# The adaLN pieces' quadrant sums by a two-column product, and three banks for the first mixer's pieces

## The chip, the cores and the metric

One Trainium2 chip; the kernel runs on one core of it. The metric is device time in microseconds of one execution, lower is better. TensorE (PE) does the matmuls and the transposes, VectorE (DVE), ScalarE (ACT) and GpSimd (POOL) the rest; every DMA that matters here is issued from SyncE's queue (SP).

## The reference

Two layers of a hybrid backbone block over 512 tokens (256 context, 256 latent) of width 1024. Layer 0 mixes with gated linear attention (GLA) next to an mLSTM, layer 1 with a Mamba-2 scan, and each is followed by a convolutional SwiGLU network (FFN). Every norm is modulated by adaLN: a conditioning vector (one for the latent, one for the context) goes through SiLU and one large product per layer, and that gives a shift, a scale and a gate for the mixer and the same for the FFN.

```python
def rmsnorm(x, g):
    xf = x.astype(jnp.float32)
    y = xf * lax.rsqrt(jnp.mean(xf * xf, axis=-1, keepdims=True) + EPS)
    return (y * g.astype(jnp.float32)).astype(x.dtype)

def modulate(x, g, shift, scale):
    return rmsnorm(x, g) * (1 + scale) + shift
```

## The kernel before

**Products.** The 1024 features lie in eight blocks of 128. Each large product is done in three passes of fp32r, high·high, low·high and high·low (L180 to L182 where the result has features on partitions, L215 to L217 where it has tokens there). Weights come as raw fp32 in transfers of 1 MB (`Stream`, L140 to L175, DMA at L154): ACT copies the raw half into `wh` (L168), and DVE, or POOL in the FFN, subtracts to get `wl` (L169). Raw tiles live in two slots, so a third transfer is issued when the first tile has been read by its last reader. PSUM is split into three pools: `gps` with 4 banks for the products, `mps` with 3 for the mixers, `vps` with 1.

**adaLN pieces.** The modulation is computed in pieces of 512 columns (`mod_chunk`, L230), 20 of them, and in 8 smaller ones of 256 (`mod_part`, L243, at the start). A piece issues two raw transfers of 1 MB (L236) into the *same* two raw slots as the weights, and does eight fp32 matmuls with the silu vector `spad` as the stationary operand (L239): each writes 32 rows of a bank, so that four quarters of the contraction lie in four quadrants of partitions. Then `mod_out` (L253): ACT copies the bank into `t2` (L256), PE transposes each block of 128 columns against `ident` (L259; 4 for a piece, 2 for a part), DVE adds the four quadrants (L263), adds the bias (L264), and for the scales applies the gain (L267). Both the bank of the products and that of the transposes come from the pool `psa`, by default `vps`, the single bank; L127 (column sums of squares of the norm) and L135 use it too.

**Where the pieces stand.** Six pieces of layer 0 (`fill0`: j = 4, 5, 8, 9, 6, 7) run inside the first mixer: the weight stream calls one when it starts a new raw tile. Two more are in that mixer's gates; the other twelve are for layer 1 and are spread over the rest, nine of them in the first FFN. The mixer itself goes in this order: gate products and the mLSTM's scans (L519 to L530, on 4 partitions, DVE), products of tokens (L215 to L217), then for each pair of GLA heads scores by level (L597, combined on DVE by L603), sums over the state (L672, normalised by L676 to L678), a transposition back (L684), and meanwhile products by features (L180 to L182) whose results DVE puts through a causal convolution (L336, L337, L575). These products wait for `wl`, and so for raw transfers.

**Order.** Nobody writes the order by hand: a scheduler orders each engine's instructions by the dependences and by when slots and banks come free in its own plan. The names in rows and lists are pool and number (`vps_252` is one use of the bank of `vps`; `rawm_253` the raw tile of a piece, `raw_273` one of the weights). On the engine, instructions run strictly in that order.

Of the kernel before, what the change touches and what calls it, by code (L numbers as in the profile page):

```python
# [9 lines left out]
F32 = mybir.dt.float32  # L10
# [3 lines left out]
ALU = mybir.AluOpType  # L14
AX = mybir.AxisListType

P = 128
# [34 lines left out]
def block_kernel(ctx: ExitStack, tc: tile.TileContext, A: dict, out: bass.AP):  # L52
    nc = tc.nc
    PSUM = bass.MemoryType.PSUM
    v, s, g, te = nc.vector, nc.scalar, nc.gpsimd, nc.tensor
# [5 lines left out]
    cp = ctx.enter_context(tc.tile_pool(name="cp", bufs=1))  # L61
# [12 lines left out]
    def nm(b):  # L74
        _u[0] += 1
        return f"{b}_{_u[0]}"

    def t2(shape=(P, T), dt=F32):
        return np_.tile(list(shape), dt, tag="t2", name=nm("t2"), bufs=6)
# [11 lines left out]
    def load(src, shape, dt=F32, eng=None):  # L91
        n = nm("c")
        t = cp.tile(shape, dt, tag=n, name=n)
        (eng or nc.scalar).dma_start(out=t, in_=src)
        return t
# [5 lines left out]
    def pc(name, i=0, n=1):  # L101
        o = _off[name] + i
        return prm[:, o:o + n]
# [121 lines left out]
    v.tensor_scalar(out=cth, in0=cth, scalar1=0.5, scalar2=0.5, op0=ALU.mult, op1=ALU.add)  # L225
    v.tensor_tensor(out=spad[:, :, 0:2], in0=cth.rearrange("p (k c) -> p k c", c=2), in1=cv.rearrange("p (k c) -> p k c", c=2), op=ALU.mult)
    ident = load(A["ident"], [P, P])
    comps = [[cp.tile([P, KD, 2], F32, tag=f"mod{l}_{i}", name=f"mod{l}_{i}") for i in range(6)] for l in range(2)]

    def mod_chunk(l, j, pool=rawp, psa=vps, tag="raw", n=2, bufs=None):  # L230

        ps = psa()
        w = KD // n
        for i in range(n):
            raw = pool.tile([P, w * 512], F32, tag=tag, name=nm("rawm"), bufs=bufs)
            nc.sync.dma_start(out=raw, in_=A["modw"][l, j, :, i * w * 512:(i + 1) * w * 512])  # L236
            for kk in range(w):
                k = i * w + kk
                te.matmul(out=ps[32 * (k % 4):32 * (k % 4) + 32, :], lhsT=spad[:, k, :], rhs=raw[:, kk * 512:(kk + 1) * 512],  # L239
                          start=k < 4, stop=k >= 4)  # L240
        mod_out(l, 4 * j, 4, ps, psa)

    def mod_part(q, pool, psa):  # L243

        ps = psa()[:, :256]
        raw = pool.tile([P, 2048], F32, tag="raw", name=nm("rawm"))
        nc.sync.dma_start(out=raw, in_=A["mods"][q])
        for k in range(KD):
            te.matmul(out=ps[32 * (k % 4):32 * (k % 4) + 32, :], lhsT=spad[:, k, :], rhs=raw[:, k * 256:(k + 1) * 256],
                      start=k < 4, stop=k >= 4)  # L250
        mod_out(0, 2 * q, 2, ps, psa)

    def mod_out(l, c, n, ps, psa):  # L253

        ev = t2((P, n * P))
        s.copy(out=ev, in_=ps)  # L256
        pt = psa()[:, :n * P].rearrange("p (a b) -> p a b", b=P)
        for a in range(n):
            te.transpose(pt[:, a, :], ev[:, a * P:(a + 1) * P], ident)  # L259
        col = lambda name, o: pc(name, o, n).unsqueeze(2).to_broadcast([P, n, 2])  # L260
        i, k = c // KD, c % KD
        dst = comps[l][i][:, k:k + n, :]
        v.tensor_reduce(out=dst, in_=pt.rearrange("p a (q c) -> p a c q", q=4)[:, :, 0:2, :], axis=AX.X, op=ALU.add)  # L263
        v.tensor_tensor(out=dst, in0=dst, in1=col("modb", l * 48 + c), op=ALU.add)  # L264
        if i in (1, 4):

            v.scalar_tensor_tensor(out=dst, in0=dst, scalar=1.0, in1=col("nmg" if i == 1 else "nfg", l * 8 + k), op0=ALU.add, op1=ALU.mult)  # L267
# [33 lines left out]
    def norm_mod(l, comp_sh, comp_sc, segs, r, between=lambda k, acts: None, tiles=None):  # L301
        c0, c1 = segs[0][1], segs[-1][2]
        hs = [] if tiles is None else tiles
        sh, sc = comps[l][comp_sh], comps[l][comp_sc]
        acts = lambda k: hs[k]
        for k in range(KD):
            between(k, acts)
            y = t2()
            for ci, a, b in segs:
                v.scalar_tensor_tensor(out=y[:, a:b], in0=xT[k][:, a:b], scalar=sc[:, k, ci:ci + 1], in1=r[:, a - c0:b - c0],  # L310
                                       op0=ALU.mult, op1=ALU.mult)
            if tiles is None:
                hs.append(htiles(k))
            h_, l_ = hs[k]
            for ci, a, b in segs:
                s.activation(out=h_[:, a:b], in_=y[:, a:b], func=AF.Identity, bias=sh[:, k, ci:ci + 1])  # L316
            for ci, a, b in segs:
                v.scalar_tensor_tensor(out=l_[:, a:b], in0=y[:, a:b], scalar=sh[:, k, ci:ci + 1], in1=h_[:, a:b].bitcast(F32),  # L318
                                       op0=ALU.add, op1=ALU.subtract)
        return acts  # L320
# [30 lines left out]
    with tc.tile_pool(name="stp", bufs=6) as stp:  # L351
# [18 lines left out]
                gemm_k(W0, 0, KD, acts, [(0, T)] * 4, pss0, (k - 1,))  # L370

        acts = norm_mod(0, 0, 1, SEGS, r, start)
    fill0 = [lambda j=j: mod_chunk(0, j) for j in (4, 5, 8, 9, 6, 7)]
    fill1 = [lambda j=j: mod_chunk(1, j) for j in (3, 0, 1, 4, 5, 8, 9, 6, 7, 11)]
    E.fill0, E.W0 = fill0, W0
    nrm = Norm(0, T)
# [25 lines left out]
    with ExitStack() as st:  # L402
# [3 lines left out]
        op = st.enter_context(tc.tile_pool(name="outp", bufs=1))  # L406
# [899 lines left out]
```

## Time and profile before

| | us |
|---|---|
| median of 3 runs | 1296.32 (1293.79, 1296.32, 2431.66) |
| the profiled execution | 1291.57 |
| its span on the core | 1289.4 |
| mean granted TensorE clock | 0.99 of full speed |
| PE busy | 1233.4 (96% of the span) |
| DVE busy | 942.9 (73%) |

A row of a timeline has the start and the length of a run of equal instructions in us from the span's start, the engine, the line, the operation, what it writes and reads, and in brackets how long the engine was idle before it and what ended that. PEld is the loading of the stationary operand, which overlaps PE. Starts of neighbouring PE rows say more than their lengths, since matmuls are pipelined and their recorded ends overlap.

### The profile page before, as it was taken

The page shows a single profiled execution, that of the slowest core. Times are in us where ns is not written, and L with a number is a line of the kernel's source. Part 1 is how long each engine was busy: PE and PEld are TensorE (multiplying, and loading weights), DVE is VectorE, ACT ScalarE, POOL GpSimd, SP SyncE. Part 2 cuts the span into 40 slices and gives each one's busy share as a digit, 9 for nine tenths or more (in the row PEclk, how much of TensorE's full clock was granted, in tenths as well). Part 3 has the DMA queues.
Part 4 walks back from the last instruction along what each step waited for, and adds up shares of the span by engine and source line. Part 5 has one row for each costly group of instructions (what it writes and reads, how often), then busy time and mean ns, then how long its engine had stood idle before and what let it go on. Part 6 is the DMA issues. An engine that isn't in the chain of part 4 may idle for free.

```text
span 1289.4 us, 19329 instructions
## 1 busy us (share of the span) xinstructions
PE 1233.4 (96%) x7358; PEld 1016.6 (79%) x7358; DVE 942.9 (73%) x2137; ACT 596.9 (46%) x947; POOL 385.3 (30%) x214
## 2 busy tenths in 40 slices
PE   7989999999999999999999999999999999899997
PEld 5657787876867677888888897887888888899997
DVE  5483899576658766227774478879888958999993
ACT  4463344343345434124443356656566545555553
POOL 0100000000225555226665000032232125778720
PEclk9989999999999999999999999999999999999999
DMA  9546303324436563222211225444454464545431
GB/s 374 207 173 229 116 16 103 118 91 164 171 145 247 220 262 139 98 98 98 99 66 67 98 76 164 156 140 153 126 152 111 169 243 150 200 165 183 142 131 66
DMA packets 39964, 190.96 MB, mean 148 GB/s; under 512 B 4592, under 2 KB 10552, under 8 KB 20928
## 3 DMA queue, kind: packets, MB, share of 16 engines
q1 hardware_dynamic: 36512, 185.48, 41.2%
q10 hardware_dynamic: 3360, 4.25, 1.1%
q8 instruction: 58, 0.95, 0.3%
q14 instruction: 34, 0.28, 0.1%
HBM read 188.51 MB, written 1.20 MB: 147 GB/s over the span
## 4 chain that ended last, share of the span: by engine, by line
PE 70%; DVE 19%; issue 4%; ACT 3%; DMA 3%; POOL 1%; SPq 0%; ACTq 0%; DVEq 0%; POOLq 0%
PE gps L180 13%; PE gps L181 13%; PE gps L182 13%; DVE y L829 6%; PE mps L180 5%; PE mps L182 4%; PE mps L181 4%; PE vps L239 3%; DVE ml L897 2%; PE vps L1113 1%; PE gps L215 1%; PE gps L216 1%; PE gps L217 1%; DVE y L893 1%; PE vps L1100 1%
## 5 line engine op out<-in xcount | busy, mean ns | idle before, releaser
L169 POOL TENSOR_TENSOR wl<-raw,wh 128x1024 fp32r<-128x1024 f32 x111 | 268.1, 2425 | 514.7 <-ACT wh L168 514.5
L168 ACT ACTIVATE wh<-raw 128x1024 fp32r<-128x1024 f32 x226 | 237.6, 1054 | 170.8 <-PE gps L182 108.4
L180 PE MATMUL gps<-hh,wh 128*128 128x512 f32 (+1 forms) x840 | 296.7, 354 | 7.1 <-ACT hh L316 5.4
L182 PE MATMUL gps<-hl,wh 128*128 128x512 f32 (+1 forms) x840 | 294.8, 352 | 1.6 <-DVE hl L318 1.6
L181 PE MATMUL gps<-hh,wl 128*128 128x512 f32 (+1 forms) x840 | 294.9, 351 | 1.2 <-DVE wl L169 1.1
L829 DVE SCALAR_TENSOR_TENSOR y<-mps,fcw,y 128x255 f32<-128x255 f32 (+3 forms) x576 | 223.1, 427 | 37.3 <-ACT y L823 31.0
L169 DVE TENSOR_TENSOR wl<-raw,wh 128x1024 fp32r<-128x1024 f32 x115 | 140.9, 1232 | 79.5 <-ACT wh L168 79.3
L180 PEld LDWEIGHTS gps<-hh,wh 128*128 128x128 f32 x840 | 159.2, 190 | 43.1 <-issue 11.7
L180 PE MATMUL mps<-hh,wh 128*128 128x256 f32 (+1 forms) x528 | 172.1, 326 | 10.8 <-DVE y L829 8.5
L182 PEld LDWEIGHTS gps<-hl,wh 128*128 128x128 f32 x840 | 159.5, 190 | 25.0 <-issue 4.2
L181 PEld LDWEIGHTS gps<-hh,wl 128*128 128x128 f32 x840 | 159.9, 190 | 24.1 <-issue 4.1
L181 PE MATMUL mps<-hh,wl 128*128 128x256 f32 (+1 forms) x528 | 170.6, 323 | 0.0
L182 PE MATMUL mps<-hl,wh 128*128 128x256 f32 (+1 forms) x528 | 170.6, 323 | 0.0
L180 PEld LDWEIGHTS mps<-hh,wh 128*128 128x128 f32 x528 | 100.3, 190 | 27.6 <-issue 9.3
L180 PE MATMUL gps<-mh,wh 128*128 128x256 f32 (+1 forms) x352 | 117.6, 334 | 2.7 <-ACT mh L896 2.7
L181 PE MATMUL gps<-mh,wl 128*128 128x256 f32 (+1 forms) x352 | 117.2, 333 | 0.0
L182 PE MATMUL gps<-ml,wh 128*128 128x256 f32 (+1 forms) x352 | 117.0, 333 | 0.0
L182 PEld LDWEIGHTS mps<-hl,wh 128*128 128x128 f32 x528 | 100.4, 190 | 7.5
L181 PEld LDWEIGHTS mps<-hh,wl 128*128 128x128 f32 x528 | 100.4, 190 | 7.1
L829 DVE SCALAR_TENSOR_TENSOR y<-gps,fcw,y 128x189 f32<-128x189 f32 (+3 forms) x196 | 83.3, 437 | 23.1 <-ACT y L823 19.3
L823 ACT ACTIVATE y<-mps,fcw 128x256 f32<-128x256 f32 (+1 forms) x66 | 40.6, 639 | 87.7 <-PE mps L182 87.7
L180 PEld LDWEIGHTS gps<-mh,wh 128*128 128x128 f32 x352 | 66.8, 190 | 10.0 <-ACT mh L896 2.9
(281 smaller groups left out, 1836.8 us busy)
## 6 DMA issues: line engine op xcount, KB each, us to landing
raw<-in_up SPq DMA_DIRECT2D x42, 1024.0 KB, 4.9
rawm<-in_modw SPq DMA_DIRECT2D x36, 1024.0 KB, 5.8
raw<-in_win SPq DMA_DIRECT2D x32, 1024.0 KB, 5.3
raw<-in_dn SPq DMA_DIRECT2D x20, 1024.0 KB, 4.9
raw<-in_wout SPq DMA_DIRECT2D x10, 1024.0 KB, 5.0
rawm<-in_mods SPq DMA_DIRECT2D x8, 1024.0 KB, 14.0
R<-crd SPq DMA_DIRECT2D x32, 256.0 KB, 4.3
rawm<-in_modw SPq DMA_DIRECT2D x8, 512.0 KB, 5.1
```

The source lines that it names most:

```text
L168: s.activation(out=hi[:, :n], in_=rw, func=AF.Copy)
L169: self.eng(u).tensor_tensor(out=lo[:, :n], in0=rw, in1=hi[:, :n].bitcast(F32), op=ALU.subtract)
L180: te.matmul(out=ps, lhsT=lhi, rhs=rhi, start=first, stop=False)
L181: te.matmul(out=ps, lhsT=llo, rhs=rhi, start=False, stop=False)
L182: te.matmul(out=ps, lhsT=lhi, rhs=rlo, start=False, stop=last)
L215: te.matmul(out=ps, lhsT=ah[:, sl], rhs=hi[:, c:c + 512], start=k == 0, stop=False)
L216: te.matmul(out=ps, lhsT=ah[:, sl], rhs=lo[:, c:c + 512], start=False, stop=False)
L217: te.matmul(out=ps, lhsT=al[:, sl], rhs=hi[:, c:c + 512], start=False, stop=k == nk - 1)
L239: te.matmul(out=ps[32 * (k % 4):32 * (k % 4) + 32, :], lhsT=spad[:, k, :], rhs=raw[:, kk * 512:(kk + 1) * 512], start=k < 4, stop=k >= 4)
L823: s.activation(out=y, in_=ps, func=AF.Identity, scale=fcw[:, ti * 10 + 4:ti * 10 + 5], bias=fcw[:, ti * 10 + 9:ti * 10 + 10])
L829: v.scalar_tensor_tensor(out=o, in0=i, scalar=fcw[:, ti * 10 + wi:ti * 10 + wi + 1], in1=o, op0=ALU.mult, op1=ALU.add)
L897: part = lambda ya=ya, h_=h_, l_=l_: ep.tensor_tensor(out=l_, in0=ya, in1=h_.bitcast(F32), op=ALU.subtract)
```

## The change

A tile `quads` of 128 x 2 is built once: column c of it has a one at each partition whose number is c in its quadrant of 32. The four transposes per piece become four fp32 products with a block of the copied bank as the stationary operand and `quads` as the two moving columns; they give the sum over quadrants at once. The DVE reduction is gone, and the bias is added straight from PSUM. Second, the six pieces of `fill0` take their banks from `mps` in place of `vps`. Behind the new lines the numbers of the changed kernel are three higher (L239 is L242, L259 is L262), and from L264 on two higher.

```diff
     ident = load(A["ident"], [P, P])
+
+    quads = cp.tile([P, 2], F32, tag="quads", name="quads")
+    v.tensor_reduce(out=quads, in_=ident.rearrange("p (q c) -> p c q", q=4)[:, 0:2, :], axis=AX.X, op=ALU.add)
...
         s.copy(out=ev, in_=ps)
-        pt = psa()[:, :n * P].rearrange("p (a b) -> p a b", b=P)
+        pt = psa()[:, :2 * n].rearrange("p (a b) -> p a b", b=2)
         for a in range(n):
-            te.transpose(pt[:, a, :], ev[:, a * P:(a + 1) * P], ident)
+            te.matmul(out=pt[:, a, :], lhsT=ev[:, a * P:(a + 1) * P], rhs=quads, start=True, stop=True)
...
-        v.tensor_reduce(out=dst, in_=pt.rearrange("p a (q c) -> p a c q", q=4)[:, :, 0:2, :], axis=AX.X, op=ALU.add)
-        v.tensor_tensor(out=dst, in0=dst, in1=col("modb", l * 48 + c), op=ALU.add)
+        v.tensor_tensor(out=dst, in0=pt, in1=col("modb", l * 48 + c), op=ALU.add)
...
-    fill0 = [lambda j=j: mod_chunk(0, j) for j in (4, 5, 8, 9, 6, 7)]
+    fill0 = [lambda j=j: mod_chunk(0, j, psa=mps) for j in (4, 5, 8, 9, 6, 7)]
```

SP's and POOL's order is the same in both kernels. PE's and DVE's differ in the first mixer. On PE, where the sixth piece of `fill0` (the raw tiles `rawm_253` and `rawm_254`) computes, before: it stands between the scores of the first pair of heads (L597) and products by features.

```order
L597 MATMUL mps_208_1130<-b4_207_1123 128x128
L597 MATMUL mps_209_1131<-b4_207_1123 128x128
L239 MATMUL vps_252_1357<-rawm_253_1358,spad_98 32x512 [waits DMAHW6_49]
L239 MATMUL vps_252_1357<-rawm_253_1358,spad_98 32x512 x3
L239 MATMUL vps_252_1357<-rawm_254_1364,spad_98 32x512 [waits DMAHW7_49]
L239 MATMUL vps_252_1357<-rawm_254_1364,spad_98 32x512 x3
L180 MATMUL gps_250_1354<-hh_35_246,wh_181_1020 128x512
L181 MATMUL gps_250_1354<-hh_35_246,wl_182_1021 128x512
```

The same piece on PE in the changed kernel: L686 is the old L684, the transposition back of the first pair of heads, and L599 the old L597.

```order
L182 MATMUL gps_272_1473<-hl_88_502,wh_265_1419 128x512
L686 MATMUL mps_245_1318<-c_3_104,b4_232_1251 128x128 [waits DVE_49]
L686 MATMUL mps_245_1318<-c_3_104,b4_232_1251 128x128
L686 MATMUL mps_246_1324<-c_3_104,b4_232_1251 128x128 x2
L599 MATMUL mps_248_1331<-qk_101_578 128x128 [waits Activation_49]
L599 MATMUL mps_249_1332<-qk_101_578 128x128
L242 MATMUL mps_252_1346<-rawm_253_1347,spad_98 32x512 [waits DMAHW6_49,DVE_49]
L242 MATMUL mps_252_1346<-rawm_253_1347,spad_98 32x512 x3
L242 MATMUL mps_252_1346<-rawm_254_1353,spad_98 32x512 [waits DMAHW7_49]
L242 MATMUL mps_252_1346<-rawm_254_1353,spad_98 32x512 x3
L262 MATMUL mps_256_1361<-quads_106,t2_255_1359 128x2 [waits DVE_49,Activation_49]
L262 MATMUL mps_256_1361<-quads_106,t2_255_1359 128x2 x3
```

It now stands behind the transposition back and the second pair's first scores, and it waits for DVE too, which sets its bank free; the next raw tile of weights, `raw_273`, takes the slot of `rawm_253`.

On DVE, the splits of that raw tile and the next (`wl_275`, `wl_283`, `wl_292`), before: they stand among the decay products of the first pair of heads, ahead of the state's sum (L659).

```order
L626 TENSOR_TENSOR b4_222_1218<-cum10_118_663 128x2x128
L647 TENSOR_TENSOR t2_227_1241<-t2_227_1241,qk_100_584 128x512
L169 TENSOR_TENSOR wl_275_1489<-raw_273_1486,wh_274_1488 128x1024 [waits DMAHW0_49]
L628 TENSOR_TENSOR b4_222_1218<-b4_222_1218,qk_100_584 128x1024 [waits Activation_49]
L169 TENSOR_TENSOR wl_283_1544<-raw_273_1486,wh_282_1543 128x1024
L169 TENSOR_TENSOR wl_292_1601<-raw_290_1598,wh_291_1600 128x1024 [waits DMAHW1_49,Activation_49]
L659 TENSOR_TENSOR t2_231_1260<-mps_230_1255,c_hblk_528 128x512 [waits PE_49]
```

The same splits on DVE in the changed kernel; L605 is the old L603 (the second pair's scores by level), L338, L339 and L577 the old L336, L337 and L575 (convolution).

```order
L339 SCALAR_TENSOR_TENSOR t2_267_1447<-gps_264_1418,c_2_86,t2_267_1447 128x2x255 [waits DVE_49]
L605 COPY_PREDICATED ao_247_1330<-lev_90_518,mps_271_1462 128x512 [waits PE_49]
L169 TENSOR_TENSOR wl_275_1477<-raw_273_1474,wh_274_1476 128x1024 [waits DMAHW0_49,Activation_49]
L577 SCALAR_TENSOR_TENSOR mk0_193_1058<-t2_268_1451,t2_267_1447 128x512 [waits Activation_49]
L338 SCALAR_TENSOR_TENSOR t2_276_1504<-gps_272_1473,c_2_86,t2_276_1504 128x2x255 [waits Activation_49]
L605 COPY_PREDICATED ao_247_1330<-lev_90_518,mps_279_1518 128x512 [waits PE_49]
L339 SCALAR_TENSOR_TENSOR t2_276_1504<-gps_272_1473,c_2_86,t2_276_1504 128x2x255 [waits DVE_49]
L605 COPY_PREDICATED ao_247_1330<-lev_90_518,mps_280_1519 128x512 [waits PE_49]
L169 TENSOR_TENSOR wl_283_1532<-raw_273_1474,wh_282_1531 128x1024
L577 SCALAR_TENSOR_TENSOR mq1_190_1055<-t2_277_1508,t2_276_1504 128x512 [waits DMAHW7_49,DMAHW4_49,Activation_49]
```

They have moved behind the whole normalisation of the first pair of heads, into the second pair's scores and the convolutions.

## Rows read from the trace of the kernel before

**Rows 1.** The page's part 1: busy time, share of the span, instructions by engine.
```profile
PE 1233.4 (96%) x7358; PEld 1016.6 (79%) x7358; DVE 942.9 (73%) x2137; ACT 596.9 (46%) x947; POOL 385.3 (30%) x214
```

**Rows 2.** Five stretches: length, busy time by engine, granted clock, DMA share, GB/s.
```profile
core 0: us, PE busy (x) PEld busy (x) DVE busy (x) ACT busy (x) POOL busy (x), PEclk, DMA share, GB/s
85.40:92.00 6.60, 6.53 (x20) 3.90 (x21) 6.57 (x15) 2.97 (x5) 0.00 (x0) 0.52 0.52 166
100.00:130.00 30.00, 30.00 (x149) 21.09 (x149) 8.07 (x13) 9.20 (x14) 0.00 (x0) 1.00 0.65 218
170.00:180.00 10.00, 10.00 (x48) 8.17 (x47) 9.83 (x30) 5.25 (x7) 0.00 (x0) 1.00 0.00 0
180.00:222.00 42.00, 40.90 (x258) 32.54 (x258) 41.94 (x69) 19.97 (x27) 0.00 (x0) 1.00 0.16 54
376.00:740.00 364.00, 364.00 (x1686) 286.70 (x1685) 221.47 (x516) 131.01 (x175) 178.89 (x95) 1.00 0.38 136
```

**Rows 3.** Weight loads of two lines: ns min/median/max, first and last start.
```profile
L259 PEld LDWEIGHTS vps<-c,t x72: 137/140/143, 61.9 to 1107.9; 128*128 128x128 f32 x72
L127 PEld LDWEIGHTS vps<-ones,t x48: 186/192/338, 12.7 to 1280.8; 128*128 128x128 f32 x48
```

**Rows 4.** Timeline of PE and its weight loads: narrow products, and one piece's transposes.
```profile
11.21 0.97 PEld L127 LDWEIGHTS vps<-ones,acc 128*128 128x128 f32 x8 [3.35 <-DVE acc L283]
17.74 0.41 PEld L135 LDWEIGHTS vps<-c,ry 128*128 128x128 f32 x4 [0.84 <-PE mps L259]
...
61.94 0.66 PE L259 MATMUL vps<-c,t 128*128 128x128 f32 x4
62.35 0.49 PE L181 MATMUL gps<-hh,wl 128*128 128x512 f32 x1
```

**Rows 5.** Timeline of DVE and PE around the third and fourth pieces.
```profile
84.51 0.68 DVE L525 TENSOR_TENSOR_SCAN mk<-ones,mk 4x256 f32<-4x256 f32 x1
85.22 0.19 DVE L263 TENSOR_REDUCE mod<-vps 128x8 f32<-128x32 f32 x1
85.47 1.94 PE L239 MATMUL vps<-rawm,spad 128*32 128x512 f32 x8 [2.88 <-DVE mod L263]
86.73 2.35 DVE L169 TENSOR_TENSOR wl<-raw,wh 128x1024 fp32r<-128x1024 f32 x2
98.23 2.35 DVE L169 TENSOR_TENSOR wl<-raw,wh 128x1024 fp32r<-128x1024 f32 x2
106.81 1.06 PE L239 MATMUL vps<-rawm,spad 128*32 128x512 f32 x8
```

**Rows 6.** DMA issues on SP's queue in the first mixer, and a transfer's landing.
```profile
89.11 0.33 SPq L154 DMA_DIRECT2D raw<-in_win  x1
95.95 4.99 SPq L236 DMA_DIRECT2D rawm<-in_modw  x2
138.01 86.24 SPq L154 DMA_DIRECT2D raw<-in_win  x7
...
142.84 1.06 ACT L168 ACTIVATE wh<-raw 128x1024 fp32r<-128x1024 f32 x1 [1.27 <-DMA raw<-in_win]
```

**Rows 7.** Timeline of PE and DVE around the sixth piece and its raw slots.
```profile
136.89 1.92 PE L239 MATMUL vps<-rawm,spad 128*32 128x512 f32 x16
161.27 1.23 DVE L169 TENSOR_TENSOR wl<-raw,wh 128x1024 fp32r<-128x1024 f32 x1 [3.12 <-ACT wh L168]
169.72 0.60 PE L259 MATMUL vps<-c,t 128*128 128x128 f32 x4
170.08 0.48 PE L180 MATMUL gps<-hh,wh 128*128 128x512 f32 x1
179.28 0.60 PE L684 MATMUL mps<-c,b 128*128 128x128 f32 x4
184.01 1.16 PE L597 MATMUL mps<-b 64*128 64x128 f32 x8 [0.41 <-DVE ao L603]
237.75 0.60 PE L651 MATMUL mps<-c,t 128*128 128x128 f32 x4
```

## The prediction

> **What bounds the kernel now.** I read the page's engine shares first: PE is busy 1233.4 us, 96% of the span [rows 1], so all idle time of PE together is about 56 us, and a change pays only if it shortens PE's own work or one of its few waits. The table of stretches says where those are. From 376 to 740 us PE has no idle time at all, 1686 matmul records in 364.00 us, 0.216 us each [rows 2]; nine of the twenty pieces stand there, and work given to PE there is paid in full, while work taken from DVE there is worth nothing. The first mixer, where the six moved pieces stand, is different: at 85.40 to 92.00 the granted clock is 0.52, and at 180 to 222 PE and DVE are both nearly full (40.90 and 41.94 of 42.00) [rows 2]. Last I read the timelines of DVE, PE and SP around the pieces of that mixer, since there the change moves instructions.
>
> **The cost of the new sum.** A piece's four transposes hold PE from 61.94 to the next product at 62.35: 0.41 us [rows 4], 0.10 each, one pass. An ordinary fp32 product is two records, each with a weight load of its own, so the new sum is 8 loads of a 128x128 block with 2 columns behind each. No row shows a two-column product. The nearest has plain fp32 loads and few columns: L127, 8 loads, 0.97 us from the first start to the last end [rows 4]; one load lasts 0.192 [rows 3], so the pitch is (0.97 - 0.19) / 7 = 0.111. I take that: 8 x 0.111 = 0.89 per piece, 0.48 more than now, and for 20 pieces **+9.6**. Bounds: the load of L259 lasts 0.140 and that of L127 0.192 [rows 3]; if nothing overlaps, 8 x 0.192 = 1.54, +1.13 a piece, +22.6. From below, the four loads of L135 take 0.41 in all, (0.41 - 0.14) / 3 = 0.09 apart [rows 4], which gives 8 x 0.09 = 0.72, +6.2; if the second pass with the same block cost nothing, 4 x 0.10 = 0.41, and the change is 0; less than that only if the loads vanish behind neighbouring products, at most -0.41 x 20 = -8.2. The L127 row is the likeliest because operand, type and number of passes are the same. The 8 small parts have half of each, +0.24, but lie in the start, where PE waits 3.35 before L127 [rows 4]: **+0.5** rather than 1.9, which is the price without that cover.
>
> The trace's pitch is 0.111 us for a load. The Trainium skill, page "TensorE: Matmul & The Clock Gate", section "LDWEIGHTS (loading the stationary operand)", has a load take the number of columns over 1.2, in ns; that is 107 ns for 128 columns, whatever the moving side is, and it speaks against the change: by it the sum would be 8 x 0.107 - 0.41 = +0.45 a piece, an estimate of +8.9 for 20.
>
> **The removed reductions.** 28 reductions at 0.19 (one stands at 85.22 [rows 5]) are 5.3 us of DVE. Most lie where PE is full [rows 2] and bring nothing; some stand between a piece and its bank or in the stretch with DVE full at 180 to 222: **-1**, between 0 and -5.3. Building `quads` is one more reduction, early, when DVE has yet to wait for data: 0, and 0.2 if that cover is gone.
>
> **What the three banks free.** The third piece's first matmul stands on PE at 82.6, but starts at 85.47 after 2.88 of idle; its releaser is the second piece's reduction on DVE at 85.22, which stands in DVE's queue behind the mLSTM's scans (the last starts at 84.51) [rows 5]. With one bank in `vps` the third piece can have it only then. After that idle the clock is 0.52 for 6.60 us, which loses 6.60 x 0.48 = 3.2 [rows 2]. With three banks of `mps`, the third piece's bank was left long before by other work: no wait, no half clock, 2.88 + 3.2 = -6.1. Given back in part at the fourth piece: its second raw tile is issued at 100.6 (the end of the row 95.95, 4.99, less 0.33 [rows 6]), when DVE has ended the splits that start at 98.23 (98.23 + 2.35 = 100.58 [rows 5]); these follow a raw tile issued at 89.11 [rows 6], when the splits at 86.73 had ended (89.08 [rows 5]), behind the same scans. Scans and splits don't move. The issue could come 1.9 earlier at best, at 98.7, since only DVE's waiting for PE's sum shrinks. A transfer takes 4.8 from issue to use (138.01 to 142.84 [rows 6]): it lands at 103.5. PE read it at 106.81 [rows 5]; 6.1 earlier is 100.7. So PE waits 2.8 there: net -3.3, and if the clock falls again behind this wait, less. I take **-3**, between -7 (no new wait, and something at the second piece) and -0.5.
>
> **What the sixth piece's move costs.** In the old order its 16 records run at 136.89, and SP issues the next raw tile at 138.01, when the first slot is read [rows 6, 7]. Its splits are done by 162.5 (the row at 161.27 [rows 7] is the last of three). In the new order the piece stands behind the first pair's transposition back, which is at 179.28 now [rows 7]; it holds its raw slots for all that time, and what is queued behind that issue on SP is every later weight of this mixer. Without the three splits (3 x 1.2) in DVE's queue ahead of it, the transposition could come some 3.6 earlier, at 175.7. But PE's 40 products between 170.08 and 179.28 (9.2 us, no idle [rows 2, 7]) need the weights that are now late; by the order 11 of them have theirs. 11 x 0.23 = 2.5 us fill PE to about 172.6, less what moved ahead of it, 171.1; it then waits to 175.3 or so: 4.2 of idle. The piece ends at about 178, the raw tile is issued at 179, is there 4.8 later, ACT's copy takes 1.06 [rows 6], the split 1.2, and it has convolutions and scores ahead of it in DVE's queue: 189.5. Up to about 183 PE has scores and the few products; idle 6.5. Together 10.7, less the 1.1 that stand there now [rows 2]: 9.6. Part of it is filled by the second pair's scores, which come forward (L597 takes 1.16 for 8 [rows 7]; some 16 are free, 2.3): **+7** at the end of that product at 237.75 [rows 7]. Bounds 0, if DVE, full there at 41.94 of 42.00, ends the stretch anyway, and +10. After such idles the clock was at 0.52 for 6.60 us once, at a cost of 3.2 [rows 2]; I take **+2** for two waits, between 0 and +5.
>
> **Sum.** +9.6 + 0.5 - 1 - 3 + 7 + 2 = +15.1. The profiled execution took 1291.57, the median is 4.7 above it, and the two shorter runs average 1295.1; I add the sum to these: 1295 + 15 = **1310** (on the profiled execution 1306.7).
>
> **The rivals.**
> A, narrow passes are cheap. The loads are done while neighbouring products stream, which take 0.216 each [rows 2], and a pass costs between nothing and half of the pitch, 0.055. For it: two of 512 columns are hardly any streaming. Against it: 0.111 and 0.10 as pitches of every load in [rows 4]. The term is then -8.2 to +0.6 and the sum -3.2 to +5.6 (parts at 0): 1292 to 1301, at its lower end not slower. It decides from 0.02 us a pass, where 20 x (8 x 0.02 - 0.41) = -5.0 cancels the other terms. The Trainium skill, same page, section "Wait — 56ns, not 53.3ns?", has the time from start to start never below about 25 ns however few the columns; by that the term would be an estimate of -4.2. No run here shows it.
> B, the sixth piece's move costs nothing, because DVE and not PE ends the stretch (41.94 of 42.00 [rows 2]). Against it: DVE's three splits come into that stretch. 7 and 2 fall away: +6.1, 1301.
> C, nothing of a load overlaps, 0.192 each: +22.6 + 1.9 in place of +9.6 + 0.5, sum +29.5, 1325. For it: the loads' lengths in [rows 3]; against it the pitches in [rows 4]. It makes the kernel slower by over 2% (26 us) from about 0.18 us a pass.
> D, both A and B: the banks' gain stays and the new sum is cheap: 9 less than A, -12 to -3, 1283 to 1292.
>
> **How the numbers follow.** Chances: forecast 0.56, A 0.17, B 0.16, C 0.06, D 0.05. The forecast's own range is 1301 to 1319 (terms at mid-way to their bounds). The range of **1294 to 1319** leaves out C, D, a tenth of the forecast and the lowest fifth of A; B is inside. A difference of about 2% (26 us) is what a measurement can tell here. Faster by over 2% (under 1270) no case gives: 0.01. Slower by over 2% (over 1322): most of C and the forecast's upper end, 0.05. Within 2%: 0.94.
>
> **What would show it.** In the changed profile: L262 with 8 records a piece, at a pitch near 0.11, and eight in about 0.9 us in the stretch without idle. No wait of about 2.9 us of the third piece's L242 on DVE at 82 to 86, and full clock behind it. A wait for a raw tile at the fourth piece's second half, near 101. L242 of the sixth piece behind L686 at 175 to 178, PE idle ahead of it, and the raw issue on SP at 179 in place of 138. L653 (the old L651) at 238 to 248. The forecast is wrong if L262's records are 0.03 apart, or if the products of the first pair's time find their weights all the same.

## The result, and the profile after

The changed kernel takes 1313.01 us (median), the kernel before 1294.51 in the same comparison: a ratio of 1.0151, interval 1.0133 to 1.017; one run of the kernel before, at 2431.66 us, is left out of the ratio. It is 1.5% slower; the forecast was 1310, within 1294 to 1319. The profiled execution has a span of 1308.0 us, 18.6 more than before.

The page of the changed kernel, its busy time by engine, which answers to [rows 1]:

```profile
PE 1247.2 (95%) x7454; PEld 1032.3 (79%) x7454; DVE 936.4 (72%) x2110; ACT 597.1 (46%) x947; POOL 384.5 (29%) x214
```

PE has 13.8 us more of busy time and 96 instructions more: 96 transposes have become 192, two for each product, which I call its two passes. Its idle time has grown from 56 to 61 us. DVE has lost 6.5 us, and the kernel is no faster for it. So PE's busy time is the larger part, waits the smaller; but in the busy time there are also stretches at half clock.

Where the 18.6 us arise can be read by the starts of the same PE instruction in both traces:

| what starts on PE | before | after | late by |
|---|---|---|---|
| first piece's matmuls (L239, now L242) | 54.71 | 59.67 | 5.0 |
| four transposes at the end of the pieces' stretch (L558, now L560) | 129.70 | 132.92 | 3.2 |
| second pair's transposes of keys (L651, now L653) | 237.75 | 249.45 | 11.7 |
| transposes behind the mLSTM (L763, now L765) | 316.95 | 328.95 | 12.0 |
| column sums behind the first FFN (L127) | 757.34 | 775.67 | 18.3 |
| last product of three passes (L182) | 1279.14 | 1297.67 | 18.5 |

The first two of these rows, in the kernel before and in the changed one:

```profile
54.71 1.06 PE L239 MATMUL vps<-rawm,spad 128*32 128x512 f32 x8 [0.40 <-DMA rawm<-in_modw]
129.70 0.60 PE L558 MATMUL mps<-c,mq 128*128 128x128 f32 x4
...
59.67 1.07 PE L242 MATMUL mps<-rawm,spad 128*32 128x512 f32 x8 [0.30 <-DMA rawm<-in_modw]
132.92 0.60 PE L560 MATMUL mps<-c,mq 128*128 128x128 f32 x4
```

Three places make it: the start (+5.0), the first mixer's second half (+8.5), and the stretch up to the end of the first FFN (+6.3). Between the first two, from 54.71 to 129.70, the changed kernel makes up 1.8.

**The new sum.** Weight loads and matmuls of L262 in the trace of the changed kernel (ns min/median/max, as in [rows 3]), and two sums in the FFN, where PE has no idle time:

```profile
L262 PEld LDWEIGHTS vps<-quads,t x96: 186/192/192, 318.9 to 1128.3; 128*128 128x128 f32 x96
...
440.45 0.95 PE L262 MATMUL vps<-quads,t 128*128 128x2 f32 x8
441.26 0.47 PE L181 MATMUL mps<-hh,wl 128*128 128x512 f32 x1
454.59 0.95 PE L262 MATMUL vps<-quads,t 128*128 128x2 f32 x8
455.40 0.47 PE L182 MATMUL mps<-hl,wh 128*128 128x512 f32 x1
```

The same two pieces before:

```profile
438.54 0.60 PE L259 MATMUL vps<-c,t 128*128 128x128 f32 x4
438.89 0.48 PE L182 MATMUL mps<-hl,wh 128*128 128x512 f32 x1
452.00 0.60 PE L259 MATMUL vps<-c,t 128*128 128x128 f32 x4
452.35 0.48 PE L182 MATMUL mps<-hl,wh 128*128 128x512 f32 x1
```

A sum holds PE 0.81 us (440.45 to 441.26) where the transposes held it 0.35: 8 loads at 0.10, not 4. That is +0.46, for 20 pieces +9.2.

**The sixth piece.** PE, SP and the table of stretches in the changed kernel, which answer to [rows 2, 6, 7]:

```profile
178.75 1.12 PE L686 MATMUL mps<-c,b 128*128 128x128 f32 x4 [4.01 <-DVE b L680]
182.55 2.49 PE L242 MATMUL mps<-rawm,spad 128*32 128x512 f32 x16
185.75 1.05 PE L262 MATMUL mps<-quads,t 128*128 128x2 f32 x8 [0.71 <-ACT t L259]
...
184.25 51.75 SPq L154 DMA_DIRECT2D raw<-in_win  x7
...
core 0: us, PE busy (x) PEld busy (x) DVE busy (x) ACT busy (x) POOL busy (x), PEclk, DMA share, GB/s
170.00:190.00 20.00, 14.55 (x100) 10.55 (x100) 17.57 (x45) 6.49 (x9) 0.00 (x0) 0.83 0.24 87
190.00:222.00 32.00, 31.56 (x183) 25.18 (x182) 31.62 (x51) 17.66 (x21) 0.00 (x0) 1.00 0.27 89
```

The piece runs at 182.55 in place of 136.89, the weights behind it are issued at 184.25 in place of 138.01, PE waits 4.01 us ahead of the transposition back, and the clock is at 0.83 of full speed in these 20 us. From 190 on PE is as full as before.

**The third piece.** PE and ACT around it in the changed kernel, which answer to [rows 5]:

```profile
86.47 1.07 PE L242 MATMUL mps<-rawm,spad 128*32 128x512 f32 x8
97.09 1.05 PE L262 MATMUL mps<-quads,t 128*128 128x2 f32 x8 [1.98 <-ACT t L259]
104.54 1.06 PE L242 MATMUL mps<-rawm,spad 128*32 128x512 f32 x8
...
95.50 1.06 ACT L629 ACTIVATE b<-b 128x1024 f32<-128x1024 f32 x1 [2.72 <-DVE b L628]
96.47 0.57 ACT L259 COPY t<-mps 128x512 f32<-128x512 f32 x1
96.93 1.06 ACT L629 ACTIVATE b<-b 128x1024 f32<-128x1024 f32 x1
...
97.00:102.00 5.00, 4.91 (x19) 4.06 (x20) 4.77 (x10) 3.00 (x4) 0.00 (x0) 0.66 0.65 262
```

The wait of 2.88 us ahead of the third piece's matmuls is gone. Ten microseconds later PE waits 1.98 us for that same piece's copy on ACT, which stands there behind an exponential (L629) that waits for DVE; and the clock falls behind that wait: 0.66 over 97 to 102.

**The start.** DVE in the changed kernel:

```profile
6.76 0.17 DVE L230 TENSOR_REDUCE quads<-c 128x2 f32<-128x8 f32 x1 [1.29 <-DMA c<-in_ident]
6.84 0.17 DVE L225 TENSOR_SCALAR cth<-cth 128x16 f32<-128x16 f32 x1
```

The reduction that builds the columns stands in DVE's queue ahead of the silu, and waits 1.29 us for `ident`. The first column sum on PE (L127, 11.21 in [rows 4]) starts at 11.92.

### The profile page after: what moved, and what is told of

The parts are those of the page before. It is cut to its first block, busy times and chain, and to the rows that moved or that the text cites. A ratio compares the mean times of both kernels' runs of the same rounds, so it can differ in the third digit from the quotient of the medians.

```text
span 1308.0 us, 19497 instructions
## 1 busy us (share of the span) xinstructions
PE 1247.2 (95%) x7454; PEld 1032.3 (79%) x7454; DVE 936.4 (72%) x2110; ACT 597.1 (46%) x947; POOL 384.5 (29%) x214
## 4 chain that ended last, share of the span: by engine, by line
PE 69%; DVE 18%; issue 4%; DMA 4%; ACT 3%; POOL 1%; ACTq 0%; SPq 0%; POOLq 0%; DVEq 0%
PE gps L180 13%; PE gps L181 13%; PE gps L182 13%; DVE y L831 6%; PE mps L180 4%; PE mps L181 4%; PE mps L182 4%; PE vps L242 2%; DVE ml L899 2%; PE vps L1115 1%; PE mps L599 1%; DVE wl L169 1%; DMA rawm<-in_modw 1%; DVE y L895 1%; PE gps L215 1%
## 5 line engine op out<-in xcount | busy, mean ns | idle before, releaser
L180 PE MATMUL gps<-hh,wh 128*128 128x512 f32 (+1 forms) x840 | 297.8, 356 | 7.1 <-ACT hh L318 5.0
L182 PE MATMUL gps<-hl,wh 128*128 128x512 f32 (+1 forms) x840 | 294.9, 353 | 1.6 <-DVE hl L320 1.6
L180 PEld LDWEIGHTS gps<-hh,wh 128*128 128x128 f32 x840 | 160.0, 191 | 43.5 <-issue 11.3
L180 PE MATMUL mps<-hh,wh 128*128 128x256 f32 (+1 forms) x528 | 172.2, 326 | 10.1 <-DVE y L831 9.0
L182 PEld LDWEIGHTS gps<-hl,wh 128*128 128x128 f32 x840 | 159.7, 190 | 24.9 <-issue 4.2
L182 PE MATMUL mps<-hl,wh 128*128 128x256 f32 (+1 forms) x528 | 170.6, 323 | 0.0
L180 PEld LDWEIGHTS mps<-hh,wh 128*128 128x128 f32 x528 | 100.3, 190 | 26.9 <-issue 9.3
L180 PE MATMUL gps<-mh,wh 128*128 128x256 f32 (+1 forms) x352 | 117.1, 333 | 2.7 <-ACT mh L898 2.7
L182 PE MATMUL gps<-ml,wh 128*128 128x256 f32 (+1 forms) x352 | 116.4, 331 | 0.0
L182 PEld LDWEIGHTS mps<-hl,wh 128*128 128x128 f32 x528 | 100.5, 190 | 7.3
L180 PEld LDWEIGHTS gps<-mh,wh 128*128 128x128 f32 x352 | 66.3, 188 | 10.0 <-ACT mh L898 2.9
```

What stands on the lines that cost most here:

```text
L180: te.matmul(out=ps, lhsT=lhi, rhs=rhi, start=first, stop=False)
L182: te.matmul(out=ps, lhsT=lhi, rhs=rlo, start=False, stop=last)
```

## The experiments

**The two halves apart.** First the new sum alone: the six pieces stay on the single bank.

```diff
-    fill0 = [lambda j=j: mod_chunk(0, j, psa=mps) for j in (4, 5, 8, 9, 6, 7)]
+    fill0 = [lambda j=j: mod_chunk(0, j) for j in (4, 5, 8, 9, 6, 7)]
```

> The new sum alone; the six pieces of the first mixer stay on the single bank. My theory from the trace of the changed kernel: the two halves of the change are separate. The sum costs 0.47 us for each of 20 pieces (+9.4) and about +5 at the start; the third piece's wait of 2.9 us on DVE and the half clock behind it stay, the sixth piece stays early (its raw issue near 140 us). So +14 over the kernel before, about 1309. Rival: the late sixth piece comes with the new sum and not with the banks; then about +18, as the whole change, 1313.

It took 1306.24 us, against 1292.88 for the kernel before in that comparison: 1.0098, 1.0072 to 1.0124. Its span is 1301.7, 12.3 more than before. The sixth piece stays early. So the two halves can be separated, and 12 us of the 18.6 belong to the sum with its start. This kernel waits for the third piece's bank, as the kernel before does; PE, and the stretch behind that wait:

```profile
90.40 1.07 PE L242 MATMUL vps<-rawm,spad 128*32 128x512 f32 x8 [3.08 <-DVE mod L266]
...
90.40:97.00 6.60, 6.60 (x35) 4.55 (x39) 6.60 (x13) 3.10 (x5) 0.00 (x0) 1.00 0.69 226
```

The wait is 3.08 us, but the clock behind it stays at 1.00, where it was 0.52 before. So the half clock that the prediction counted as part of this wait's price need not follow it.

Then the banks alone, on the kernel before, with transposes:

```diff
-    fill0 = [lambda j=j: mod_chunk(0, j) for j in (4, 5, 8, 9, 6, 7)]
+    fill0 = [lambda j=j: mod_chunk(0, j, psa=mps) for j in (4, 5, 8, 9, 6, 7)]
```

> The three banks alone, transposes and reductions as before. My theory: the third piece's wait goes (-4), and the sixth piece moves behind the transposition back and costs +9: +5 over the kernel before, about 1299. Rival B of the prediction: the sixth piece's move costs nothing by itself; then -4, about 1290.

1300.9 us, 1.006 (1.0037 to 1.0084), span 1298.3. The banks alone make the kernel slower by 8 us, and by the ratios the two halves add up to about the whole: 0.98% and 0.60%, against 1.51%. In its trace, PE and SP at the sixth piece:

```profile
176.19 1.12 PE L684 MATMUL mps<-c,b 128*128 128x128 f32 x4 [3.99 <-DVE b L678]
179.99 2.63 PE L239 MATMUL mps<-rawm,spad 128*32 128x512 f32 x16
...
181.83 51.39 SPq L154 DMA_DIRECT2D raw<-in_win  x7
```

The wait of 4 us, the late piece and the late issue are those of the changed kernel, without any two-column product. Rival B, that this move costs nothing, is out.

**The sixth piece.** The whole change, with this one piece on the bank it had:

```diff
-    fill0 = [lambda j=j: mod_chunk(0, j, psa=mps) for j in (4, 5, 8, 9, 6, 7)]
+    fill0 = [lambda j=j: mod_chunk(0, j, psa=vps if j == 7 else mps) for j in (4, 5, 8, 9, 6, 7)]
```

> The whole change, but the sixth piece keeps the single bank of vps. My theory: its place on PE is again ahead of the transposition back, the raw issue is back near 140 us, PE's idle of 4 us and the half clock at 177 to 184 are gone: 9 less than the whole change, about 1304. Rival: that stretch is set by DVE whatever the order is; then 1313.

1305.25 us, 1.0102 (1.0067 to 1.0136), span 1302.8: 5.2 less than the whole change by the spans, 6.3 by the two ratios (1.0151 - 1.0102 = 0.0049 of 1293), where my theory had 9; the ratios leave some 5 us of uncertainty. Its stretch at the sixth piece, and the raw issue:

```profile
174.00:186.00 12.00, 12.00 (x64) 10.05 (x64) 11.11 (x31) 6.40 (x10) 0.00 (x0) 1.00 0.01 1
...
142.70 87.62 SPq L154 DMA_DIRECT2D raw<-in_win  x7
```

No idle time, full clock, and the issue at 142.70 in place of 184.25. In the changed kernel the same stretch has PE at 7.27 of 12.00 and the clock at 0.72. The starts on PE give the price more sharply than whole runs: from the four transposes at 129.70 of the kernel before to those at 237.75 it takes 108.05 us there, 116.53 in the changed kernel and 108.97 in this one. In the traces of all twelve kernels this stretch is 116.3 to 117.7 us in the six whose sixth piece is on the three banks, and 108.0 to 109.0 in the six where it isn't.

The same edit on the kernel before, so that five pieces have three banks and the transposes stay:

```diff
-    fill0 = [lambda j=j: mod_chunk(0, j) for j in (4, 5, 8, 9, 6, 7)]
+    fill0 = [lambda j=j: mod_chunk(0, j, psa=vps if j == 7 else mps) for j in (4, 5, 8, 9, 6, 7)]
```

> Transposes as before, five of the six pieces on the three banks, the sixth on vps. My theory: the banks' gain without the price of the sixth piece, -4: about 1290, the shortest of all. Rival: what the third piece gains is given back later in the mixer, then no difference to the kernel before, 1294 to 1295.

1294.73 us, 1.0008 (0.9989 to 1.0028), span 1288.7: no difference. Against the banks alone this is 9.6 less by the spans and 6.2 by the medians, for the sixth piece; by the stretch above it is 8.3 (116.29 and 107.99). And the banks' gain of 4 us that I expected is not there: from 54.71 to 129.70 of the kernel before, 74.99 us, this kernel takes 73.57, so 1.4 are gained. PE and ACT show where the rest goes:

```profile
96.02 0.66 PE L259 MATMUL mps<-c,t 128*128 128x128 f32 x4 [3.54 <-ACT t L256]
...
93.10 1.06 ACT L627 ACTIVATE b<-b 128x1024 f32<-128x1024 f32 x1 [2.80 <-DVE b L626]
94.44 1.06 ACT L627 ACTIVATE b<-b 128x1024 f32<-128x1024 f32 x1 [0.28 <-DVE b L626]
95.40 0.57 ACT L256 COPY t<-mps 128x512 f32<-128x512 f32 x1
```

The third piece's matmuls no longer wait. Its copy stands in ACT's queue behind two exponentials, which wait for decays that DVE makes behind the same scans. PE, ahead of the scans now, waits 3.54 us for the copy: the stall has moved down the same piece.

**The moved stall.** To see whether that costs the gain, the third piece's copy and sum are written behind the fourth piece's products, on the last kernel:

```diff
-    def mod_chunk(l, j, pool=rawp, psa=vps, tag="raw", n=2, bufs=None):
+    def mod_chunk(l, j, pool=rawp, psa=vps, tag="raw", n=2, bufs=None, pend=None, defer=False):
...
+        if defer:
+            pend.append((l, 4 * j, 4, ps, psa))
+            return
         mod_out(l, 4 * j, 4, ps, psa)
+        while pend:
+            mod_out(*pend.pop())
...
-    fill0 = [lambda j=j: mod_chunk(0, j) for j in (4, 5, 8, 9, 6, 7)]
+    pend = []
+    fill0 = [lambda j=j: mod_chunk(0, j, psa=vps if j == 7 else mps, pend=pend, defer=j == 8) for j in (4, 5, 8, 9, 6, 7)]
```

> As the kernel with transposes, five pieces on the three banks and the sixth on vps, but the third piece's copy and sum are written after the fourth piece's products. In the kernel without this, PE waits 3.54 us at 92.5 to 96.0 for ACT's copy of the third piece, which stands in ACT's queue behind two exponentials (L627) that wait for DVE behind the scans, and the clock halves behind it. My theory: this is where the banks' gain goes. Then the wait goes, and PE runs until it needs the fourth piece's second raw tile (the wait that the prediction put at 2.8 us) or the products of the next weights: 0 to 5 less, about 1291. Rival: everything behind the scans is late by the same amount, so that another wait of 3 us takes its place within 20 us; then 1293 to 1295, no difference.

1291.5 us, against 1292.39: 0.9984, 0.997 to 0.9998. That is 1 us shorter than the kernel before by the medians and 2 by the ratio, just outside its uncertainty, and the shortest of all. PE in its trace, and the whole stretch:

```profile
98.71 1.07 PE L239 MATMUL mps<-rawm,spad 128*32 128x512 f32 x8 [1.68 <-DMA rawm<-in_modw]
104.92 1.07 PE L239 MATMUL mps<-rawm,spad 128*32 128x512 f32 x8 [1.05 <-DMA rawm<-in_modw]
...
84.00:105.00 21.00, 18.27 (x93) 12.39 (x89) 15.14 (x28) 8.73 (x13) 0.00 (x0) 1.00 0.63 225
```

The wait for ACT is gone, the clock stays full, and two waits for the fourth piece's raw tiles come up, 1.68 + 1.05 = 2.73 us. The prediction had put 2.8 there, all of it at the second tile, which has 1.05; the 1.68 at the first tile it did not have. While PE waited for ACT, neither wait was there. At 129.70 of the kernel before, this one is 1.9 us early (127.82), and the kernel without the deferral 0.6 late (130.33), so 2.5 us are gained in the traces. By whole runs the two are not clearly apart, 0.9984 (0.997 to 0.9998) and 1.0008 (0.9989 to 1.0028). Both theories are half right: a part is gained, a part is a new wait within 20 us.

**What the price of the sum is.** One pass in place of two: the copied bank and the columns are fp32r.

```diff
-    quads = cp.tile([P, 2], F32, tag="quads", name="quads")
-    v.tensor_reduce(out=quads, in_=ident.rearrange("p (q c) -> p c q", q=4)[:, 0:2, :], axis=AX.X, op=ALU.add)
+    qf = cp.tile([P, 2], F32, tag="qf", name="qf")
+    quads = cp.tile([P, 2], F32R, tag="quads", name="quads")
+    v.tensor_reduce(out=qf, in_=ident.rearrange("p (q c) -> p c q", q=4)[:, 0:2, :], axis=AX.X, op=ALU.add)
+    v.tensor_copy(out=quads, in_=qf)
...
-        ev = t2((P, n * P))
+        ev = t2((P, n * P), F32R)
```

> The whole change, but the copied bank and the two columns are fp32r, so that each product is one pass with one weight load; this rounds the piece to fp32r before the sum. My theory: the price is the second load. Four loads take 0.4 us as the transposes did, so 20 x 0.45 = 9 less than the whole change and some 1 to 2 at the start: about 1303. Rival: the price hangs on something else of the product (its operand from ACT, or the write of two columns); then 1313.

1304.78 us, 1.0088 (1.0055 to 1.012), span 1302.0. Some 8 us less than the whole change by the two ratios (1.0151 - 1.0088 = 0.0063 of 1293). Then 128 moving columns in place of 2:

```diff
-    quads = cp.tile([P, 2], F32, tag="quads", name="quads")
-    v.tensor_reduce(out=quads, in_=ident.rearrange("p (q c) -> p c q", q=4)[:, 0:2, :], axis=AX.X, op=ALU.add)
+    quads = cp.tile([P, P], F32, tag="quads", name="quads")
+    g.memset(quads, 0.0)
+    v.tensor_reduce(out=quads[:, 0:2], in_=ident.rearrange("p (q c) -> p c q", q=4)[:, 0:2, :], axis=AX.X, op=ALU.add)
...
-        pt = psa()[:, :2 * n].rearrange("p (a b) -> p a b", b=2)
+        pt = psa()[:, :n * P].rearrange("p (a b) -> p a b", b=P)
...
-        v.tensor_tensor(out=dst, in0=pt, in1=col("modb", l * 48 + c), op=ALU.add)
+        v.tensor_tensor(out=dst, in0=pt[:, :, 0:2], in1=col("modb", l * 48 + c), op=ALU.add)
```

> The whole change, but 128 columns move where 2 did (126 of them zeros). My theory: the loads set the pitch, as in the row of L127, and the columns cost nothing: 0.11 us a pass, no difference to the whole change (within 2 us). Rival: the streaming counts, 126 columns more at 0.216 us for 512 is 0.05 a pass, 8.5 us for 20 pieces.

1309.66 us, 1.0133 (1.0092 to 1.0173), span 1308.3, as the whole change. The sums in the FFN, one pass first:

```profile
409.85 0.50 PE L264 MATMUL vps<-quads,t 128*128 128x2 f32 x4
410.22 0.48 PE L181 MATMUL mps<-hh,wl 128*128 128x512 f32 x1
```

and with 128 columns:

```profile
453.87 1.05 PE L263 MATMUL vps<-quads,t 128*128 128x128 f32 x8
454.68 0.48 PE L182 MATMUL mps<-hl,wh 128*128 128x512 f32 x1
```

Four loads with 2 columns behind each take 0.37, eight with 2 columns 0.81, eight with 128 columns 0.81. The number of loads sets the price, 0.09 to 0.10 each, and 128 columns cost no more than 2. The transposes had 4 loads, with 128 columns behind each, 0.35. That settles rival A.

**The start.** The changed kernel is 5.0 us late at 54.7, where the prediction had 0.5. Two runs asked why. In one the columns are built on GpSimd:

```diff
-    v.tensor_reduce(out=quads, in_=ident.rearrange("p (q c) -> p c q", q=4)[:, 0:2, :], axis=AX.X, op=ALU.add)
+    g.tensor_tensor(out=quads, in0=ident[:, 0:2], in1=ident[:, 32:34], op=ALU.add)
+    g.tensor_tensor(out=quads, in0=quads, in1=ident[:, 64:66], op=ALU.add)
+    g.tensor_tensor(out=quads, in0=quads, in1=ident[:, 96:98], op=ALU.add)
```

> The whole change, but the two columns are built by three additions on GpSimd and not by a reduction on DVE. In the changed kernel that reduction waits 1.29 us on DVE for the transfer of ident, ahead of the silu and of the norm's sums, and the first column sum on PE starts 0.7 us later. My theory: the 0.7 us come back. If the half clock at 19.7 to 26.6 us of the changed kernel hangs on this lateness, another 3.4 us: -4. Rival: the half clock there comes from the narrow products themselves; then only -0.7.

1312.64 us, 1.0142 (1.0107 to 1.0177): no difference. L127 starts at 11.46, 0.46 earlier, so the reduction's wait on DVE is a part of the 0.7; but by the first piece PE is 0.9 later than in the changed kernel (60.62), and the gain doesn't show in all. In the other the eight parts keep transposes and reductions:

```diff
+        if n == 2:
+            pt = psa()[:, :n * P].rearrange("p (a b) -> p a b", b=P)
+            for a in range(n):
+                te.transpose(pt[:, a, :], ev[:, a * P:(a + 1) * P], ident)
+        else:
+            pt = psa()[:, :2 * n].rearrange("p (a b) -> p a b", b=2)
+            for a in range(n):
+                te.matmul(out=pt[:, a, :], lhsT=ev[:, a * P:(a + 1) * P], rhs=quads, start=True, stop=True)
...
+        if n == 2:
+            v.tensor_reduce(out=dst, in_=pt.rearrange("p a (q c) -> p a c q", q=4)[:, :, 0:2, :], axis=AX.X, op=ALU.add)
```

> The whole change, but the eight parts at the start (256 columns each) keep their transposes and reductions. In the changed kernel PE is 5.0 us late by the first piece (54.7 us), where the prediction gave 0.5. My theory: the parts pay in full, 8 x 0.24 = 1.9, since PE has no idle time to take them at most of their places; then it is 2 to 3 us late there and 2 to 3 less in all, about 1310. Rival: the lateness is the clock (half from 19.7 to 26.6 us, where it was full) and the reduction for the columns; then 4 to 5 late, and no difference in all, 1313.

1311.31 us, 1.014 (1.011 to 1.017), span 1309.7. At 54.7 it is 4.1 late: my theory had 2 to 3, the rival 4 to 5. That is 0.9 less than the changed kernel, but two kernels whose start has the same code differ by more: the whole change is 5.0 late and the one with the sixth piece on `vps` 6.4. And 1.014 against 1.0151 tells nothing. The rows of the parts tell more; one in the changed kernel, and one before:

```profile
29.80 0.50 PE L262 MATMUL mps<-quads,t 128*128 128x2 f32 x4
30.16 0.48 PE L180 MATMUL gps<-hh,wh 128*128 128x512 f32 x1
...
28.86 0.38 PE L259 MATMUL mps<-c,t 128*128 128x128 f32 x2
29.00 0.48 PE L180 MATMUL gps<-hh,wh 128*128 128x512 f32 x1
```

A part takes 0.36 where it took 0.14, 0.22 more, at four of the eight places (29.80, 32.37, 39.52, 51.85), where products stand on both sides: 0.9. At three others PE waits for ACT ahead of the sum. So 0.9 of the parts' 1.9 can be read as paid. The clock in the stretch from 12 to 30 us is the larger part. The kernel before:

```profile
12.00:30.00 18.00, 14.37 (x110) 8.74 (x109) 10.73 (x38) 5.74 (x12) 0.00 (x0) 0.91 1.01 416
```

the changed one:

```profile
12.00:30.00 18.00, 14.71 (x94) 10.10 (x94) 8.09 (x27) 5.32 (x10) 0.00 (x0) 0.72 1.01 414
```

and with the parts transposed:

```profile
12.00:30.00 18.00, 14.08 (x85) 9.32 (x86) 8.54 (x30) 4.97 (x10) 0.00 (x0) 0.73 1.01 415
```

18 us at 0.72 and not 0.91 lose 18 x 0.19 = 3.4. With 0.7 for the reduction and 0.9 for the parts that makes the 5.0. But the kernel with transposes throughout and five pieces on three banks has 0.82 there, and is 2.05 late at 54.7 with the old code in its start; the one-pass kernel, with the new sum, has 0.91. If what the clock loses from 0 to 54 us beyond the kernel before (length times what is missing to full speed, over 0 to 12, 12 to 30 and 30 to 54) is taken off each kernel's lateness at 54.7, the three kernels with transposes and more banks keep 0.2 to 0.3, the six with the new sum throughout 1.1 to 1.8, the one with columns from GpSimd 0.8 and the one with transposed parts 0.5. So some 1.5 of the 5.0 is the new sum's own. There is one profile of each. What sets the clock in this stretch, and whether the new sum has a share in it, stays open.

**Both good halves.** The one-pass sum on the kernel with the deferred third piece (the edits of both, as shown above, together):

> The last one, with the two-column sum in one pass (fp32r operands, which rounds the pieces to fp32r before the sum) in place of transposes and reductions. My theory: four loads cost what four transposes cost, and the reductions are gone: 0 to 2 less than the same kernel with transposes, or 1 more by the reduction on DVE ahead of the norm. Rival: the start's lateness of the new sum (5 us in the changed kernel) has its own cause; then 3 to 5 more.

1295.46 us, 1.0025 (1.0009 to 1.0041): some 4 us more than the same kernel with transposes. At 54.7 it is 5.0 late, where the transposed one is 2.0 late; at 129.7 it is level with the kernel before, the transposed one 1.9 ahead. So the rival's number holds: with this sum the start is 3 us later here even with one pass, and the reductions that are gone don't cover it. Of these 3 us the clock has 1.7 (0.93 over 30 to 54 us, where the transposed kernel has 1.00), the sum 1.3.

## Why the prediction was right, point by point

The time (1310 against 1313.01) and the direction came out. Of the terms some did and some did not.

| term | forecast | found | from |
|---|---|---|---|
| new sum, 20 pieces | +9.6 | +9.2 | 0.81 - 0.35 in the FFN; runs with one pass and with 128 columns |
| start: parts and columns | +0.5 | +5.0 | start of the first piece; some 1.5 parts and columns, 3.4 clock, whose cause is open |
| three banks | -3 | about 0 in all, -0.4 to -1.4 in their stretch | five pieces on three banks: 1.0008, span -0.7; with the new sum, spans of 1302.8 and 1301.7 |
| sixth piece, with the clock | +7 + 2 | +8 | lateness 3.2 to 11.7 less its own sum; 8.3 between two kernels with transposes; 6 to 7 by the ratios |
| DVE's reductions | -1 | not seen apart | no run removes them alone |

The column found does not add up to the 18.5: its rows come from different pairs of kernels, and the stretch of the pieces, where the banks were to help, is 4.1 us shorter in these two traces, without the sums, for reasons that are mostly not the banks'.

**The new sum** was right in mechanism and size. The row of L127 in [rows 4] was the right one to lean on, since it is two passes of plain fp32 loads; the pitch of 0.10, where 0.111 was taken, stands on eight in 0.81. The Trainium skill, page "TensorE: Matmul & The Clock Gate", section "LDWEIGHTS (loading the stationary operand)", counts a load by its own columns: 107 ns for 128. The trace comes near it in the time from start to start, 0.81 / 8 = 0.101 us with 2 moving columns and with 128; the recorded length of one load is 0.19 and overlaps the next. Of the Trainium skill's lower bound of about 25 ns between starts, which was quoted beside rival A, these runs show nothing, since the loads take the time here.

**The sixth piece** was right in place and in size, and wrong in one step. The late raw issue was forecast at 179 and is at 184.25; the wait ahead of the transposition at 4.2 and is 4.01. The second wait of 6.5 us at 183 to 189.5 didn't come: from 170 to 222 PE's idle time rises from 1.10 [rows 2] to 5.45 + 0.44 = 5.89, by 4.8, where the forecast had 9.6 before scores were counted against it. In its place the clock costs more: 20 us at 0.83 lose 3.4, and 2 were allowed. 4.8 + 3.4 = 8.2, and with the piece's own 0.46 that is the 8.5.

**The banks** were the step that failed, although the trace gives back what they were to bring. From 54.71 to 129.70 the changed kernel makes up 1.8 us and pays five sums (2.3) there, so 4.1 come from elsewhere, where 3 were forecast. That the number fits is luck: the new sum alone, on one bank, makes up 1.3 and so 3.6 there too. The stretch of the kernel before, of the changed one, and of the sum alone:

```profile
54.00:129.70 75.70, 72.08 (x331) 46.94 (x330) 38.80 (x67) 35.50 (x53) 0.00 (x0) 0.95 0.62 210
```
```profile
57.00:132.90 75.90, 73.44 (x355) 49.49 (x354) 38.57 (x63) 35.95 (x53) 0.00 (x0) 0.98 0.61 214
```
```profile
57.00:133.50 76.50, 71.98 (x356) 48.58 (x355) 38.75 (x63) 35.64 (x53) 0.00 (x0) 1.00 0.63 215
```

PE is idle for 3.6, 2.5 and 4.5 us, and the clock costs 75.7 x 0.05 = 3.8, 75.9 x 0.02 = 1.5 and nothing. With the sum on one bank the wait stays and the half clock does not come; with three banks PE is idle for 2.0 us less than that, and 1.5 of it are lost again to the clock. The banks' own share is what two kernels differ by that have them or not: 0.4 us in this stretch with the new sum (73.65 and 73.25), 1.4 with transposes (74.99 and 73.57), and nothing that can be measured in whole runs. The forecast took 6.1 us from the third piece's wait and gave 2.8 back at the fourth piece's raw tile. It asked what is late next on SP, and did not ask it of ACT: behind the third piece's matmuls comes its copy, and ACT's queue had an exponential ahead of it (two with transposes), which hangs on the scans through DVE's decays. There the stall came back as 1.98 us (3.54 with transposes). A wait for the fourth piece's raw tiles exists, 2.73 us for both, but only shows when the copy is out of the way. And 3.2 of the 6.1 was the half clock, which does not always follow such a wait.

**The start** was mis-sized. I let the parts be hidden by PE's wait ahead of L127, and the columns by DVE's. About half of the parts are (0.9 of 1.9 can be read as paid). The columns aren't: DVE was idle early, but the silu and the norm's sums stood behind the reduction, which waited 1.29 us for `ident`. The clock in the start was not looked at. Some 1.5 us of the 5.0 are the new sum's own; the 3.4 of the clock stay unexplained, and kernels with transposes and an unchanged start lose up to 1.9 us to it too.

**What I left out** is the clock in the first FFN: of the 6.3 us in the stretch up to its end, eleven sums are 5.1. The rest lies at the norm ahead of it, where both kernels wait for ACT (L180 by 2.13 us) and the clock is low behind it; the changed kernel, and the same 8 us of the kernel before:

```profile
374.00:382.00 8.00, 5.69 (x16) 4.40 (x17) 6.58 (x18) 4.53 (x10) 0.00 (x0) 0.57 0.73 307
```
```profile
360.00:368.00 8.00, 5.77 (x22) 4.53 (x23) 6.98 (x21) 4.47 (x10) 0.00 (x0) 0.80 0.89 376
```

PE is as idle as before, and the clock costs 8 x 0.23 = 1.8 more. Why it does is not shown, but the extra comes back: in the six kernels with two passes this stretch takes 446.1 to 447.4 us, in the four with transposes 438.8 to 440.4.

The total came out because the start (4.5 more than forecast) and this clock (1.8) were missed on one side, while on the other the stretch of the pieces gave 1.1 more, the sixth piece cost 1.0 less (8.5 less its own sum is 8.0) and the sum 0.4 less. Without the -1 for the reductions the forecast and these add up to 19.9, and 18.6 were measured; the reductions may be in the 1.3, but no run shows that. So misses of some 6 us one way met misses of 2.5 the other, and that the sum of them stayed within the range is in part luck. What was right for its own reasons is the sum, 9.2, and the sixth piece, about 8.

## What to carry to other kernels

A product with few moving columns was priced here by its weight loads: count passes times blocks, and swap a one-pass transpose for a two-pass fp32 product only where PE has time for it, however much it spares another engine. When a wait is taken away by a spare buffer, walk on along the same piece of work and look at each queue it enters (here ACT's), since work that was late for the same reason takes the wait over. And a buffer that lives longer than planned can hold a second one that it was loaded from: look at the raw slots behind every piece that an order moves.

## What was not expected of the hardware

The price of the products was the same with 2 moving columns and with 128: eight loads took 0.81 us with either. The granted clock behind a wait was not the same from kernel to kernel: 0.52 over 6.60 us behind 2.88 of idle time on PE in the kernel before, 1.00 over 6.60 us behind 3.08 in the kernel with the new sum alone.
